# A combined logarithm and exponential table, loaded ahead of the norms and the gate decays of a hybrid decoder step

## The chip, the cores and the metric

The kernel runs on one core of a Trainium2 chip. The metric is the device time in microseconds (us) of one execution; lower is better. The engines of the core are told apart as in the profile: PE is TensorE (PEld its weight loads), DVE is VectorE, ACT is ScalarE, POOL is GpSimd, SP is SyncE, which here only issues transfers.

## The reference, cut to what matters

One decoder layer is computed for a prompt of 256 tokens and for 8 samples of 4 tokens, 288 token columns in all. A state-space branch (four groups) and a gated linear attention branch (GLA, four heads) run in parallel, are merged by sigmoid gates, and are followed by cross-attention and a convolutional feed-forward part. Every matrix product with a weight is float32 in and out. What the change touches are the norms and the logarithm of the GLA gates:

```python
# after the input product, per state-space group of 512 channels
u = u * lax.rsqrt(jnp.mean(u * u, axis=-1, keepdims=True) + EPS)
# per GLA head of 512 channels
o = o * lax.rsqrt(jnp.mean(o * o, axis=-1, keepdims=True) + EPS) * p['gla_norm']
# GLA decays
glog = jax.nn.log_sigmoid((g_lr @ p['w_gla_gate']) + p['b_gla_gate']) / GATE_TAU
# merge, and the norms ahead of cross-attention and of the feed-forward part
merged = jax.nn.sigmoid(gate_a) * branch_a + jax.nn.sigmoid(gate_b) * branch_b
x32 * lax.rsqrt(jnp.mean(x32 * x32, axis=-1, keepdims=True) + EPS)
```

## The kernel before, in words

**The weight products.** All activations are held transposed, channels on the partitions and the 288 tokens along the free axis. `proj_w` takes a weight two row blocks of 128 and 256 columns at a time. Each such piece is one transfer of 256 KB on SP's queue into a ring of six buffers `raw`; `wsplit` rounds it on ACT to `whi` (line 103) and takes the remainder on DVE as `wlo` (line 105), each into a ring of five; then PE runs twelve products of 128x288 on it (lines 148, 149 and 153). This is one step of a main generator. The results lie in two alternating pairs of PSUM tiles, `acc0` and `acc1`; ACT or DVE reads them out when a projection is done.

**The order of the work.** `weave` runs a main generator (projections) and takes, between its steps, steps of a background generator (a scan) in a fixed ratio. Eight units follow each other: four state-space groups, then four GLA heads. During unit `n` the scan of unit `n` is woven into the input projection of unit `n+1` and the output projection of unit `n-1` (`project`). In unit 0 three tile pairs of the half gate `gate_early` stand at the end of the main generator, in unit 2 one more pair; their tangents go to `gq` (line 1275). The program text gives a priority; a scheduler that simulates the engines writes the final order of each engine's queue at build time, apart from instructions that are pinned with `keep_in_program_order`, which puts an instruction behind the one that was traced before it on its engine. In a queue each engine runs in order and waits where an operand is missing.

**The norms.** Each scan ends in `finish`: the sum of squares is split into two parts `sqh` and `sql` (for all but the last unit), PE sums over the partitions with a product with ones (line 989, into a tile of the three-buffer PSUM ring `mm`), and `rstd_from` computes the reciprocal root on ACT as exp(-0.5 ln(x)) in two activations, lines 232 (logarithm) and 233 (exponential). DVE and ACT then make the normed operand `un`, which the output projection uses 16 main steps into the next unit. `rstd_of` does the same for the two full-width norms. The first products of the next scan (lines 761 to 771) take tiles of the same ring `mm`; the third of them takes the one that holds the sum of squares.

**Activation tables.** ACT computes logarithm, exponential, tangent, SiLU and root from a table set that must be loaded; copies, squares, identity and relu need no particular set. The build puts a load ahead of an activation whose function is not in the set that is active, taking a set of its own choice. `S.preload_act_table_set(LNEXP)` is an explicit load of the set named `natural_log_exp_and_others`; the kernel before has one, at its start (line 285). The tangent (lines 650, 658, 1275, 1302 and 1418) serves the SiLU and the sigmoids, and the exponential also the decays of the state-space scan (lines 834, 835) and those of GLA (`decays`, lines 1045 to 1068).

Of the kernel before, what the change touches and what calls it, by code (L numbers as in the profile page):

```python
# [8 lines left out]
F32 = mybir.dt.float32  # L9
# [7 lines left out]
P = 128  # L17
# [6 lines left out]
T = SEQ + NS  # L24
# [12 lines left out]
LNEXP = "natural_log_exp_and_others"  # L37
# [5 lines left out]
def hybrid_step(ctx: ExitStack, tc: tile.TileContext, I: dict, O: list):  # L43
# [3 lines left out]
    V, S, G = nc.vector, nc.scalar, nc.gpsimd  # L47
    MM, TR = nc.tensor.matmul, nc.tensor.transpose

    def pool(name, bufs=1, **kw):  # L50
        return tc.tile_pool(name=name, bufs=bufs, reuse_waits="tile", **kw)

    const = ctx.enter_context(pool("const"))
# [12 lines left out]
    def mm_tile():  # L66
        return ps.tile([P, 512], F32, tag="mm", bufs=3, name="mm")
# [7 lines left out]
    ones = const.tile([P, P], F32, name="ones")  # L75
    V.memset(ones, 1.0)
    epsc = const.tile([P, 3], F32, name="epsc")
    V.memset(epsc[:, 0:1], EPS)
    V.memset(epsc[:, 1:2], 4.0 * EPS)
    fold4 = const.tile([P, NS], F32, name="fold4")  # L80
# [85 lines left out]
    def proj(w, c0, ncol, X, nk, cons, row0=0, alloc=acc_tiles):  # L166
        def load(k0, kn):
            return wload(rows_of(w, row0, k0, kn, c0, ncol))
        return proj_w(load, ncol, X, nk, cons, alloc=alloc)
# [26 lines left out]
    def split_from(hi, lo, src, scale):  # L196
        S.activation(hi, src, ACT.Identity, scale=scale)
        V.scalar_tensor_tensor(lo, src, scale, hi, ALU.mult, ALU.subtract)

    def split(hi, lo, src):  # L200
        S.copy(hi, src)
        V.tensor_tensor(lo, src, hi, ALU.subtract)
# [23 lines left out]

    def two(u, n):
        return lambda k: (u[:, k, :], u[:, n + k, :])

    def rstd_from(pl, ssq, n, four=False):  # L230
        r = pl.tile([P, T], F32, tag="rstd", bufs=1, name="rstd")
        S.activation(r, ssq, ACT.Ln, scale=1.0 / n, bias=epsc[:, 1:2] if four else epsc[:, 0:1])
        S.activation(r, r, ACT.Exp, scale=-0.5)
        return r
# [345 lines left out]
    def a4(name):  # L580
        return pa.tile([P, 4, T], F32, tag="a4", bufs=4, name=name)
# [4 lines left out]
    def b2r(name):  # L586
        return pa.tile([P, 512], F32R, tag="b2", bufs=10, name=name)
# [23 lines left out]
    def e2(name):  # L611
        return pa.tile([P, 2, T], F32, tag="e2", bufs=7, name=name)
# [366 lines left out]
    fin = []  # L979

    def finish(u, sq, gcol, four):

        if len(fin) < 7:
            sp = b2r("sqh")[:, 0:T], b2r("sql")[:, 0:T]
            split(*sp, sq)
            yield
            ssq = mm_tile()
            for w in range(2):
                MM(ssq[:, 0:T], ones.bitcast(F32R), sp[w], start=(w == 0), stop=(w == 1))
        else:  # L990
            ssq = mm_tile()
            MM(ssq[:, 0:T], ones, sq, start=True, stop=True)
        rstd = rstd_from(pa, ssq[:, 0:T], 512, four)
        yield
        un = pa.tile([P, 8, T], F32R, tag="un", bufs=1, name="un")
        for t in range(4):
            V.tensor_tensor(u[:, t, :], u[:, t, :], rstd, ALU.mult)
            split_from(un[:, t, :], un[:, 4 + t, :], u[:, t, :], gcol[:, t:t + 1])
            if t % 2:
                yield  # L1000
        fin.append(un)
# [14 lines left out]
    def gla_proj(h, out):  # L1016
        vT, sr = a4("vT"), a4("sr")
        for j2 in range(2):
            def consv(j, a, j2=j2):
                S.copy(vT[:, 2 * j2 + j, :], a)  # L1020
            yield from proj(I["w_in"], O_V + 512 * h + 256 * j2, 256, X, KT, consv)
        vd = dumped(vT, f"v_d{h}")
        for j2 in range(2):
            def consr(j, a, j2=j2):
                silu2(a, sr[:, j2 * 2 + j, :])
            yield from proj(I["w_in"], O_R + 512 * h + 256 * j2, 256, X, KT, consr)
        eb, qe, ke, kd = e2("eb"), e2("qe"), e2("ke"), e2("kd")
        kde = pa.tile([P, 2, 2, 64], F32, tag="kde", bufs=1, name="kde")
        gw = b2("gw")[:, 0:256]
        for q in (1, 2, 3):  # L1030
            G.dma_start(out=gw[32 * q:32 * q + 16], in_=I["w_gla_gate"][:, 256 * h:256 * h + 256])
        b = kd

        def decays():

            for q in (1, 2, 3):
                S.copy(gw3[32 * q:32 * q + 16], gw[32 * q:32 * q + 16])
            V.tensor_tensor(gw3[96:112], gw[96:112], gw3[96:112], ALU.subtract)
            yield
            for k in range(2):  # L1040
                a = mm_tile()
                MM(a[:, 0:T], gw3[:, k * P:(k + 1) * P], lr3, start=True, stop=True)
                S.activation(qe[:, k, :], a[:, 0:T], ACT.Identity, bias=vec("b_gla_gate")[:, 2 * h + k:2 * h + k + 1])
            yield
            S.activation(ke, qe, ACT.Abs)
            S.activation(ke, ke, ACT.Exp, scale=-1.0)
            S.activation(ke, ke, ACT.Ln, bias=1.0)
            V.scalar_tensor_tensor(qe, qe, 0.0, ke, ALU.min, ALU.subtract)
            yield
            for k in range(2):  # L1050
                V.tensor_tensor_scan(b[:, k, :], rm_g, qe[:, k, :], 0.0, ALU.mult, ALU.add)
            yield
            S.activation(eb, b, ACT.Exp, scale=1.0 / 16.0)
            S.activation(ke, b, ACT.Exp, scale=-1.0 / 16.0)
            for s0, s1, c in ((0, SEQ, 64), (SEQ, T, NL)):
                bv = b[:, :, s0:s1].rearrange("p k (c l) -> p k c l", l=c)
                kv = qe[:, :, s0:s1].rearrange("p k (c l) -> p k c l", l=c)
                for k in range(2):
                    V.tensor_tensor(kv[:, k], bv[:, k, :, c - 1:c].to_broadcast([P, (s1 - s0) // c, c]), bv[:, k],
                                    ALU.subtract)  # L1060
            yield

            for k in range(2):
                bv = b[:, k, 0:SEQ].rearrange("p (i c l) -> p i c l", c=2, l=64)
                V.tensor_tensor(kde[:, k], qe[:, k, 0:SEQ].rearrange("p (i c l) -> p i c l", c=2, l=64)[:, :, 0, :],
                                bv[:, :, 1, 63:64].to_broadcast([P, 2, 64]), ALU.add)
            S.activation(kd, qe, ACT.Exp, scale=1.0 / 16.0)
            S.activation(kde, kde, ACT.Exp, scale=1.0 / 16.0)

        def consq(j, a):  # L1070
            V.scalar_tensor_tensor(qe[:, j, :], a, 1.0 / 16.0, eb[:, j, :], ALU.mult, ALU.mult)

        def consk(j, a):
            V.tensor_tensor(ke[:, j, :], a, ke[:, j, :], ALU.mult)
            V.tensor_tensor(kd[:, j, :], a, kd[:, j, :], ALU.mult)
            V.tensor_tensor(kde[:, j], a[:, 0:SEQ].rearrange("p (i c l) -> p i c l", c=2, l=64)[:, :, 0, :], kde[:, j],
                            ALU.mult)
        dg = decays()
        for _ in proj(I["w_in"], O_K + 256 * h, 256, X, KT, consk):
            next(dg, None)  # L1080
            yield
        yield from proj(I["w_in"], O_Q + 256 * h, 256, X, KT, consq)
        out.append((eb, qe, ke, kd, kde, vT, sr, vd))
# [182 lines left out]
            yield from proj(I["w_in"], o + 256 * j2, 256, X, KT, cons)  # L1266

    gq = []
    GH = KT // 4

    def gate_early(t, a):

        if t % 2 == 0:
            gq.append(e2("gq"))
        S.activation(gq[-1][:, t % 2, :], a, ACT.Tanh, scale=0.5)
        if t % 2:
            G.dma_start(out=ga_d[:, t - 1:t + 1, :], in_=gq[-1])

# [3 lines left out]
    def branch_a(t):  # L1282

        if t < 2 * GH:
            if t % 2 == 0:
# [3 lines left out]
        if t % 4 == 3:  # L1289
            nc.sync.dma_start(out=(mg_d if t < 2 * GH else ma_d)[:, t - 3:t + 1, :], in_=ma[:, t - 3:t + 1, :])  # L1290

# [38 lines left out]
    for n in range(8):  # L1330
        kind, i = units[n]
        scan = (ssd_scan if kind == "s" else gla_scan)(i, *outs[n][0])
        nxt = start(n + 1) if n < 7 else gate(O_GA, gate_a, GH)
        if n == 5:
            mb = bigf("mb")
        parts = [nxt, gate(O_GA, gate_early, 0, GH - 1)] if n == 0 else [steps(nxt, 16), project(n - 1), nxt]
        if n == 2:
            parts.append(gate(O_GA, gate_early, GH - 1, GH))
        weave(chain(*parts), scan, N_MAIN[n], N_BG[n], 20 if n in (2,3) else 0)
# [108 lines left out]

    def rstd_of():
        ssq = mm_tile()  # L1450
        tc.keep_in_program_order(MM(ssq[:, 0:T], ones, rst.pop(), start=True, stop=True))
        return rstd_from(pb, ssq[:, 0:T], D)

    rst = []
# [436 lines left out]
    a = acc_tiles(1)[0]  # L1891
# [64 lines left out]
```

## Time and profile before

| | us |
|---|---|
| three runs: median | 2484.65 |
| three runs: lowest and highest | 2481.55, 2485.2 |
| the profiled execution | 2484.34 |
| its span in the profile | 2482.6 |

The profiled execution lies 0.3 us under the median of the runs. Its time is 1.7 us longer than the span, which goes from the first to the last instruction. The granted TensorE clock was 0.998 over the span. Lines of the profile name the source line, the engine, the operation, the output and input tiles, and then busy time and mean duration; an "idle before" names the engine that ended the wait.

### The profile page before, as it was taken

The numbers are of one execution on the slowest core, as the hardware profiler recorded it, in microseconds if no ns is written. First come the engines' busy times: TensorE is split into PE (matmuls) and PEld (weight loads), VectorE is DVE, ScalarE is ACT, GpSimd is POOL, SyncE is SP. The second block draws the span as 40 slices with busy tenths as digits, with TensorE's granted clock in tenths as the row PEclk, the third lists the DMA queues.
The fourth block names the chain that finished last, engine by engine and source line by source line (L and its number), as shares of the span: only waits on it lengthen the run. The fifth ranks groups of instructions, "written<-read, shape, count | busy, mean of one in ns | idle before, by whom it ended". The sixth has DMA issues, their size and how long they took to land.

```text
span 2482.6 us, 52081 instructions
## 1 busy us (share of the span) xinstructions
PE 2466.9 (99%) x18766; PEld 2387.6 (96%) x18766; DVE 1769.0 (71%) x3794; ACT 1343.4 (54%) x2733; POOL 436.1 (18%) x792
## 2 busy tenths in 40 slices
PE   9999999999999999999999999999999999999998
PEld 8889999999999999999999998999999999999998
DVE  6756778896877666777666577667777676676766
ACT  6656647646464655544555545555555454554545
POOL 3102135143111010110111122402111001020012
PEclk9999999999999999999999999999999999999999
DMA  8877697787769686877777698656555555555555
GB/s 257 250 225 201 167 270 216 205 249 223 230 210 295 200 261 184 249 252 221 234 234 252 204 342 306 195 164 172 170 172 172 172 170 173 170 172 168 170 173 170
DMA packets 457075, 528.66 MB, mean 213 GB/s; under 512 B 40252, under 2 KB 403612, under 8 KB 456784
## 3 DMA queue, kind: packets, MB, share of 16 engines
q1 hardware_dynamic: 420272, 422.39, 56.6%
q0 software_dynamic: 36512, 102.93, 13.0%
q8 instruction: 147, 2.41, 0.4%
q14 instruction: 112, 0.92, 0.1%
q10 hardware_dynamic: 32, 0.01, 0.0%
HBM read 476.41 MB, written 48.76 MB: 212 GB/s over the span
## 4 chain that ended last, share of the span: by engine, by line
PE 95%; DMA 2%; issue 1%; DVE 1%; ACT 0%; POOL 0%; DVEq 0%; POOLq 0%; ACTq 0%
PE acc L149 27%; PE acc L148 27%; PE acc L153 27%; PE acc L328 2%; PE acc L329 2%; PE acc L332 2%; DMA kc<-in_cache_mem_k_dram 1%; PE mm L1239 1%; PE la L1230 1%; PE la L1576 1%; PE mm L1194 0%; DMA raw<-in_w_ssd_out_dram 0%; DMA vc<-in_cache_mem_v_dram 0%; PE la L903 0%; PE mm L924 0%
## 5 line engine op out<-in xcount | busy, mean ns | idle before, releaser
L103 ACT CAST whi<-raw 128x512 fp32r<-128x512 f32 x1464 | 899.7, 618 | 965.2 <-PE acc L149 781.7
L105 DVE TENSOR_TENSOR wlo<-raw,whi 128x512 fp32r<-128x512 f32 x1464 | 996.6, 686 | 549.2 <-ACT whi L103 536.4
L149 PE MATMUL acc<-xn,whi 128*128 128x288 f32 (+1 forms) x1936 | 541.5, 296 | 0.0
L148 PE MATMUL acc<-xn,whi 128*128 128x288 f32 (+1 forms) x1936 | 539.8, 294 | 0.3 <-ACT whi L103 0.3
L153 PE MATMUL acc<-xn,wlo 128*128 128x288 f32 (+1 forms) x1936 | 408.2, 292 | 0.0
L149 PE MATMUL acc<-hf,whi 128*128 128x288 f32 x1408 | 393.1, 296 | 0.0
L148 PE MATMUL acc<-hf,whi 128*128 128x288 f32 x1408 | 388.7, 292 | 0.0
L148 PEld LDWEIGHTS acc<-xn,whi 128*128 128x128 f32 (+1 forms) x1936 | 363.3, 188 | 5.1 <-issue 2.3
L149 PEld LDWEIGHTS acc<-xn,whi 128*128 128x128 f32 (+1 forms) x1936 | 363.7, 188 | 3.6 <-issue 0.4
L153 PEld LDWEIGHTS acc<-xn,wlo 128*128 128x128 f32 (+1 forms) x1936 | 310.4, 188 | 0.9 <-issue 0.4
L153 PE MATMUL acc<-hf,wlo 128*128 128x288 f32 x1408 | 294.5, 290 | 0.0
L149 PEld LDWEIGHTS acc<-hf,whi 128*128 128x128 f32 x1408 | 264.5, 188 | 0.0
L148 PEld LDWEIGHTS acc<-hf,whi 128*128 128x128 f32 x1408 | 264.0, 188 | 0.0
L153 PEld LDWEIGHTS acc<-hf,wlo 128*128 128x128 f32 x1408 | 226.3, 188 | 0.1
L149 PE MATMUL acc<-pr,whi 128*128 128x288 f32 x704 | 196.6, 295 | 0.0
L148 PE MATMUL acc<-pr,whi 128*128 128x288 f32 x704 | 194.8, 293 | 0.0
L1749 POOL COPY fsp<-fst 128x16 f32<-128x16 f32 x88 | 37.3, 427 | 650.7 <-DVE av L1761 431.4
L153 PE MATMUL acc<-pr,wlo 128*128 128x288 f32 x704 | 147.3, 290 | 0.0
L148 PE MATMUL acc<-un,whi 128*128 128x288 f32 x512 | 143.0, 295 | 2.5 <-ACT vT L1020 1.5
L149 PE MATMUL acc<-un,whi 128*128 128x288 f32 x512 | 142.9, 295 | 0.0
L149 PEld LDWEIGHTS acc<-pr,whi 128*128 128x128 f32 x704 | 132.3, 188 | 0.0
L148 PEld LDWEIGHTS acc<-pr,whi 128*128 128x128 f32 x704 | 132.0, 188 | 0.0
(551 smaller groups left out, 4301.9 us busy)
## 6 DMA issues: line engine op xcount, KB each, us to landing
raw<-in_w_in_dram SPq DMA_DIRECT2D x480, 256.0 KB
raw<-in_w_up_dram SPq DMA_DIRECT2D x352, 256.0 KB
raw<-in_w_down_dram SPq DMA_DIRECT2D x176, 256.0 KB
raw<-in_w_ck_dram SPq DMA_DIRECT2D x64, 256.0 KB
raw<-in_w_cv_dram SPq DMA_DIRECT2D x64, 256.0 KB
raw<-in_w_ssd_out_dram SPq DMA_DIRECT2D x64, 256.0 KB
sin<-in_state_gla_dram POOLq DMA_DIRECT2D x32, 512.0 KB, 6.2
out_dram<-sin SPq DMA_DIRECT2D x32, 512.0 KB
```

Source lines behind the costliest of these rows:

```text
L103: S.copy(hi, raw)
L105: V.tensor_tensor(lo, raw, hi, ALU.subtract)
L148: MM(a, hi[:, k, cs], xh, start=(k0 + s0 + k == 0), stop=False)
L149: MM(a, hi[:, k, cs], xl, start=False, stop=False)
L153: MM(a, lo[:, k, cs], xh, start=False, stop=(k0 + s0 + k == nk - 1))
L328: MM(accs[m], mn_hi[:, kk, ms_], hi[:, 0, :], start=(kk == 0), stop=False)
L329: MM(accs[m], mn_lo[:, kk, ms_], hi[:, 0, :], start=False, stop=False)
L332: MM(accs[m], mn_hi[:, kk, ms_], lo[:, 0, :], start=False, stop=(kk == KT - 1))
L1230: MM(osa[NS * j:NS * j + NS, :], qdm[:, k, b, :], sins[b][:, k, :], start=False, stop=(q == 1 and k == 0))
L1239: MM(a, kb[:, k * P:(k + 1) * P], vst, start=True, stop=True)
L1576: MM(ssc[NS * c:NS * c + NS, 0:P], xq[:, j, u, :], kt[:, j], start=(j == 0), stop=(j == 15))
L1749: G.tensor_copy(sp[:, :, 0:2], st.rearrange("p (b k) -> p b k", k=2))
```

## The change

A new helper `lnexp` loads the combined set explicitly. With an operand it first copies one column of it to a new scratch tile `junk1`, so that the load stands behind whatever wrote that operand. It is called in three places: in `finish` for the first seven units, behind the product with ones; in `decays`, between the absolute value and the first exponential; and in `rstd_of`, ahead of the product with ones. In `finish` of units 0 and 2 a loop is added that gives way to the main generator until the next pair of half-gate tangents has been traced, and the copy reads the last of them; in the other units it reads `sql`.

```diff
+    junk1 = const.tile([P, 1], F32, name="junk1")
...
+    def lnexp(after=None):
+
+        if after is not None:
+            S.copy(junk1, after)
+        tc.keep_in_program_order(S.preload_act_table_set(LNEXP))
...
     # finish
             for w in range(2):
                 MM(ssq[:, 0:T], ones.bitcast(F32R), sp[w], start=(w == 0), stop=(w == 1))
+            if len(fin) in (0, 2):
+                after = len(gq)
+                while len(gq) == after or len(tanhs) % 2:
+                    yield
+                lnexp(gq[-1][:, 1, 0:1])
+            else:
+                lnexp(sp[1][:, 0:1])
...
     # decays
             S.activation(ke, qe, ACT.Abs)
+            lnexp()
             S.activation(ke, ke, ACT.Exp, scale=-1.0)
             S.activation(ke, ke, ACT.Ln, bias=1.0)
...
     gq = []
+    tanhs = []
...
     # gate_early
         S.activation(gq[-1][:, t % 2, :], a, ACT.Tanh, scale=0.5)
+        tanhs.append(t)
...
     def rstd_of():
         ssq = mm_tile()
-        tc.keep_in_program_order(MM(ssq[:, 0:T], ones, rst.pop(), start=True, stop=True))
+        a = rst.pop()
+        lnexp(a[:, 0:1])
+        tc.keep_in_program_order(MM(ssq[:, 0:T], ones, a, start=True, stop=True))
```

## The prediction

> **What bounds the kernel now.** I read the head of the page first, then the waits of PE, then PE's idle time in windows, and only then the table loads on ACT, which are what the change is about.
>
> ```profile
> span 2482.6 us, 52081 instructions
> PE 2466.9 (99%) x18766; PEld 2387.6 (96%) x18766; DVE 1769.0 (71%) x3794; ACT 1343.4 (54%) x2733; POOL 436.1 (18%) x792
> ...
> PE 95%; DMA 2%; issue 1%; DVE 1%; ACT 0%; POOL 0%; DVEq 0%; POOLq 0%; ACTq 0%
> ```
>
> PE is busy for 2466.9 of 2482.6 us and carries 95% of the chain that ended last. The change takes no work from PE, so all that it can win is inside the 15.7 us in which PE is idle. ACT is idle for nearly half the span: a shorter ACT is worth nothing unless PE stood waiting for it. So the next view is what PE waited for, over the whole span (engine, line, releaser: us, times, longest).
>
> ```profile
> PE acc L148 <- ACT vT L1020: 1.5, 2, 1.1
> ...
> PE acc L148 <- DVE ma L1010: 1.0, 1, 1.0
> PE mm L771 <- ACT rstd L232: 0.8, 1, 0.8
> PE acc L148 <- ACT whi L103: 0.3, 1, 0.3
> ```
>
> Only one of these waits names a norm: line 771 waited once, 0.8 us, for the logarithm of line 232. The windows say where the idle time lies (stretch, its length, PE busy, PEld, DVE, ACT, POOL, clock, DMA share).
>
> ```profile
> 0.00:40.00 40.00, 38.87 (x191) 32.64 (x192) 27.38 (x67) 27.89 (x63) 18.61 (x50) 1.00 0.80 245
> ...
> 2440.00:2482.00 42.00, 33.21 (x261) 32.97 (x259) 25.51 (x49) 20.97 (x41) 9.63 (x15) 0.91 0.56 157
> ```
>
> ```profile
> 480.00:500.00 20.00, 19.17 (x149) 18.88 (x148) 18.86 (x41) 15.87 (x32) 0.61 (x1) 1.00 0.45 136
> ...
> 585.00:605.00 20.00, 19.69 (x154) 19.41 (x153) 14.30 (x31) 18.83 (x44) 8.75 (x13) 1.00 0.61 176
> 605.00:625.00 20.00, 18.52 (x145) 17.91 (x145) 11.73 (x23) 9.32 (x20) 13.59 (x21) 1.00 1.02 279
> 625.00:645.00 20.00, 19.02 (x165) 18.04 (x160) 19.63 (x44) 6.13 (x11) 5.19 (x9) 1.00 0.64 190
> 660.00:680.00 20.00, 20.00 (x156) 19.16 (x158) 12.03 (x23) 10.09 (x19) 0.00 (x0) 1.00 0.80 233
> 680.00:700.00 20.00, 20.00 (x158) 18.99 (x148) 16.66 (x41) 15.58 (x26) 5.18 (x8) 1.00 0.59 155
> 775.00:800.00 25.00, 25.00 (x188) 23.11 (x187) 16.18 (x28) 11.26 (x22) 3.86 (x7) 1.00 0.99 297
> ```
>
> Start (1.13 us) and tail (8.79 us) hold 9.9 of the 15.7 us, and nothing of the change is there. Of the other 5.8 us, 0.83 lie in the stretch of norm 1 (480 to 500), 0.31 + 1.48 + 0.98 = 2.77 behind norm 2 (585 to 645). Around the first GLA decays and norm 3 (680 to 700) PE has no idle time at all. The most that the whole change can win is therefore about 5.8 us, 0.23%.
>
> **The change part by part.** First the loads themselves (line, count, busy us, mean ns).
>
> ```profile
> L232 ACT ACT_TABLE_LOAD x10 | 12.8, 1283 | 0.2
> L233 ACT ACT_TABLE_LOAD x10 | 12.8, 1283 | 0.2
> ...
> L1047 ACT ACT_TABLE_LOAD x4 | 5.1, 1283 | 0.1
> L1053 ACT ACT_TABLE_LOAD x4 | 5.1, 1283 | 0.1
> ...
> L650 ACT ACT_TABLE_LOAD x1 | 1.3, 1283 | 0.0
> ...
> L286 ACT COPY epsc<-epsc 128x1 f32<-128x1 f32 x1 | 0.2, 191 | 0.0
> ```
>
> Each of ten norms loads for the logarithm and again for the exponential, each of four decays likewise: 28 loads, and four others (lines 285, 650, 1799, 1824) make 32. The set that the exponential brings holds the tangent too: no tangent loads, but the first one at line 650, which stands behind the combined set loaded at the start. So the combined set lacks the tangent, and after the change the first tangent behind a norm must load again. Counting the program: start 1, first tangent 1, decays 4, norms 0 to 6 seven, the two norms of `rstd_of` 2, norm 7 (whose branch has no `lnexp`) 2, tangents behind norms 0 to 6 seven, SiLU and root 2: 26 loads. If a preload of the set already active is dropped, norms 3 to 6 and the second `rstd_of` save five: 21. ACT thus saves 6 to 11 loads of 1.283 us and gets nine copies of about 0.19 us (price from line 286): 6 to 12 us net of 1343 us. That total is hidden; what counts is where the load sits.
>
> Norm 1, on DVE, PE and ACT (start, us, instruction, wait before it):
>
> ```profile
> 485.42 0.45 DVE L202 TENSOR_TENSOR sql<-sqa,sqh 128x288 fp32r<-128x288 f32 x1
> ...
> 488.22 1.28 ACT L232 ACT_TABLE_LOAD   x1
> ...
> 488.36 0.38 PE L989 MATMUL mm<-sql,ones 128*128 128x288 f32 x1
> ...
> 489.51 0.50 ACT L232 ACTIVATE rstd<-mm,epsc 128x288 f32<-128x288 f32 x1
> ...
> 490.07 0.33 PE L771 MATMUL mm<-ident,xsT 128*128 128x128 f32 x1 [0.83 <-ACT rstd L232]
> ```
>
> The sum of squares is complete at 488.74, the logarithm starts at 489.51, because the load runs until 489.50. The new copy needs `sql`, there at 485.87, so copy and load (1.47 us) can be through by 488; the logarithm then starts 0.77 us earlier and PE's wait shrinks by that. Queued behind copy and load are the weight casts of line 103, which PE needs several pieces later; I cost that at nothing. Term A: -0.8 us (bounds: 0 if the load stays behind the product, -0.83 at most).
>
> Norm 2, on ACT, with the last half-gate tangent and the stalls behind:
>
> ```profile
> 586.87 0.40 ACT L1275 ACTIVATE gq<-acc 128x288 f32<-128x288 f32 x1
> ...
> 588.56 1.28 ACT L232 ACT_TABLE_LOAD   x1
> 589.85 0.50 ACT L232 ACTIVATE rstd<-mm,epsc 128x288 f32<-128x288 f32 x1
> ...
> 591.54 1.28 ACT L233 ACT_TABLE_LOAD   x1
> 592.84 0.44 ACT L233 ACTIVATE rstd<-rstd 128x288 f32<-128x288 f32 x1
> ...
> 601.08 0.60 ACT L103 CAST whi<-raw 128x512 fp32r<-128x512 f32 x1
> ...
> 618.77 0.62 ACT L103 CAST whi<-raw 128x512 fp32r<-128x512 f32 x1 [3.43 <-DMA raw<-in_w_ssd_out_dram]
> 619.30 0.39 ACT L1020 COPY vT<-acc 128x288 f32<-128x288 f32 x1
> 620.95 0.62 ACT L103 CAST whi<-raw 128x512 fp32r<-128x512 f32 x1 [1.27 <-DMA raw<-in_w_ssd_out_dram]
> 621.48 0.39 ACT L1020 COPY vT<-acc 128x288 f32<-128x288 f32 x1
> ```
>
> From 588.56 to 608 ACT has not one gap: here it is the bound. The cast at 601.08 comes too late (PE's 0.3 us wait for `whi`), and because casts free the `raw` ring late, the transfers of the next projection are issued late and bunch up in a stretch whose DMA share is 1.02; two casts wait for them, and the `vT` copies queued behind these casts keep PE waiting 1.5 us for its accumulators. The norm already stands behind the tangent (586.87), so the new loop moves nothing; the first load stays where it is, and the second (591.54) goes. Everything behind it moves 1.28 us ahead, less one copy (0.19): 1.1. PE can follow by no more than that: 0.3 at the cast and the rest, 0.8 of 1.5, at the copies. The next wait, 1.0 us on `ma`, ends with a chain of transfers that moves with the rest. Term B: -1.1 us (bounds: 0 if the transfers come no earlier, -1.8 if both stalls vanish).
>
> Norm 0:
>
> ```profile
> 371.91 0.40 ACT L1275 ACTIVATE gq<-acc 128x288 f32<-128x288 f32 x1
> 372.33 1.28 ACT L232 ACT_TABLE_LOAD   x1
> 373.63 0.50 ACT L232 ACTIVATE rstd<-mm,epsc 128x288 f32<-128x288 f32 x1
> ```
>
> It too follows the last tangent at once, so the wait added there costs the copy alone, and PE shows no wait for this logarithm. The transfers of the gate pair are issued ahead of the loop as before; SP's and POOL's queues get nothing new. Norms 3 to 6, the decays and both `rstd_of`: PE idles at none of them, a shorter ACT is worth 0.
>
> The seven tangents that now reload are all behind `acc` or `cva`; the GLA ones stand in stretches like 660 to 680 and 775 to 800, where PE is never idle and ACT is busy 10.09 of 20 and 11.26 of 25 us. What each holds up is the release of one accumulator pair, wanted again one whole projection later. I take 0, with 1.3 us each as the upper bound.
>
> The sum: A -0.8, B -1.1, others 0: -1.9 us against the profiled 2484.34, which makes 2482.4; against the median of the runs, 0.3 higher, 2482.75. I say 2482.6.
>
> [...]
>
> **The rivals.** *Nothing moves.* The scheduler leaves the load of norm 1 behind the product, or the transfers at 605 to 625 are set by the DMA share of 1.02 and not by their issue. For it: that share, and that the three waits in question hold 2.6 us in all (0.8, 1.5, 0.3). Against it: the casts there did free `raw` late. Time 2484.5.
>
> *The freed ACT time unblocks more.* All of the 0.83 us and of the 2.77 us behind norm 2 go, the 0.98 us of 625 to 645 too: -3.6, 2481.0. That is what a switch worth more than its 1.28 us would do. Against it: 1.30 us from load to activation. [...] A gain over 5 us would need nearly all 5.8 us and is left almost no chance.
>
> *Reloads exposed: slower.* The tangent of each unit now waits for a load that was not there. [...] If PE waits for each of the seven, that is 7 x 1.30 = 9.1 us less 1.9: 2491.8. It decides from two exposed reloads on (2.6 against 1.9), and is over 0.2% from six on. For it: ACT runs in order, so the casts behind the tangent wait as well, and the DMA share is 0.99 in 775 to 800. Against it: idle ACT time and whole projections of slack. A rewritten queue order, which the trace of before cannot show, has the same sign and size.
>
> **How the numbers follow.** Forecast (-0.8 to -3): 0.55. Nothing moves: 0.24. More freed: 0.08. Exposed reloads or a worse order: 0.13, about half of it over 5 us. 0.2% is 5 us, about what a measurement of this kernel can tell from no change; the three runs already differ by 3.7. Faster by more than that 0.05 (an upper end of "more freed"), slower by more 0.08, within it 0.87. The range: the forecast and "more freed" with the runs' scatter give the low end, 2479.5; a few exposed reloads the high end, 2487.5.
>
> **What would show it.** Loads: 21 to 26 instead of 32, none left at line 1047, 1053 or, in norms 0 to 6, 233. Term A: PE's wait at line 771 for the logarithm falls under 0.2 us, with the load over before the product with ones ends. Term B: ACT from the norm 2 load to its first gap 1 us shorter, PE's wait for `vT` under 0.8 and for `whi` gone. Reloads: ACT loads at the first tangents near 396, 509, 663, 779, 898, 1016 and 1076, with PE full around them. I am wrong if PE's idle time outside start and tail is not about 3.9 us, or if a tangent slips between a preload and its logarithm, which would show as three loads in one norm.

## The result, and the profile after

The changed kernel takes 2500.86 us (median of 6 runs, 2497.86 to 2509.82) against 2483.78 us for the kernel before (6 runs, 2481.55 to 2485.8): a ratio of 1.0074, with a 95% interval of 1.006 to 1.0087. It is 17 us slower. The forecast was 2482.6 us, and its range ended at 2487.5.

The profiled execution of the changed kernel took 2506.51 us, 5.6 us more than its median, so its rows show somewhat more loss than a typical run has. The head of its page, its largest DMA queue (packets, MB, share of 16 engines) and its chain:

```profile
span 2504.6 us, 52086 instructions
...
PE 2476.7 (99%) x18766; PEld 2394.7 (96%) x18766; DVE 1769.6 (71%) x3794; ACT 1335.3 (53%) x2736; POOL 437.8 (17%) x792
...
q1 hardware_dynamic: 420272, 422.39, 57.7%
...
PE 92%; DMA 5%; DVE 1%; issue 1%; ACT 0%; POOL 0%; DVEq 0%; ACTq 0%; POOLq 0%; SPq 0%
```

The same queue in the kernel before:

```profile
q1 hardware_dynamic: 420272, 422.39, 56.6%
```

ACT does what the change says: it is 8.1 us less busy (1343.4 before). The engines' own instructions aren't slower: DVE is busy for 1769.6 us (1769.0 before), and a weight cast on ACT takes 620 ns (619 before). What is new is the DMA side. Packets and megabytes are the same to the last digit, and yet they occupy a larger share of a span that is itself longer. DMA has risen from 2% to 5% of the chain that ended last. PE is idle for 27.9 us instead of 15.7. Its waits after the change (engine, line, releaser: us, times, longest):

```profile
PE acc L149 <- ACT whi L104: 4.1, 2, 3.2
PE la L1652 <- DVE pms L1639: 3.5, 2, 2.4
PE acc L149 <- DVE ma L1024: 3.4, 2, 2.6
PE mm L931 <- ACT cst L632: 3.1, 1, 3.1
PE acc L149 <- ACT vT L1034: 1.2, 1, 1.2
...
PE mm L778 <- ACT rstd L239: 1.0, 1, 1.0
```

The first five have nothing to do with a norm. The last is the wait at the third tile of norm 1 (line 771 before): it was to go, and it has become 0.14 us longer (0.97 instead of 0.83). Where the time goes is in the windows (stretch, length, PE, PEld, DVE, ACT, POOL, clock, DMA share, GB/s). First the kernel before:

```profile
200.00:372.00 172.00, 172.00 (x1343) 169.17 (x1342) 126.31 (x257) 97.38 (x208) 47.65 (x96) 1.00 0.76 214
372.00:600.00 228.00, 227.17 (x1784) 220.95 (x1783) 188.13 (x407) 144.16 (x317) 81.95 (x144) 1.00 0.77 220
...
560.00:600.00 40.00, 40.00 (x311) 38.15 (x310) 25.72 (x51) 25.37 (x56) 11.33 (x18) 1.00 0.71 201
...
680.00:1150.00 470.00, 470.00 (x3541) 450.26 (x3531) 333.23 (x686) 255.99 (x471) 54.92 (x84) 1.00 0.76 235
...
1400.00:1560.00 160.00, 158.43 (x1631) 144.13 (x1630) 114.20 (x284) 77.52 (x185) 37.38 (x55) 1.00 0.85 300
```

and the changed kernel:

```profile
200.00:372.00 172.00, 171.08 (x1323) 167.32 (x1323) 124.66 (x255) 95.34 (x204) 47.60 (x96) 1.00 0.79 208
372.00:600.00 228.00, 220.57 (x1682) 212.18 (x1681) 179.38 (x388) 131.12 (x288) 76.69 (x132) 0.99 0.82 211
...
560.00:600.00 40.00, 36.80 (x261) 34.68 (x260) 26.51 (x56) 17.77 (x34) 4.72 (x7) 0.91 0.83 234
...
680.00:1150.00 470.00, 470.00 (x3542) 449.74 (x3541) 333.87 (x681) 251.12 (x468) 54.38 (x83) 1.00 0.78 236
...
1400.00:1560.00 160.00, 155.86 (x1607) 144.96 (x1605) 112.69 (x274) 77.26 (x179) 30.70 (x44) 1.00 0.86 290
```

Read the counts of PE in brackets. From 372 to 600 us PE gets through 1682 matmuls instead of 1784; at the pace of before (228 / 1784 = 0.128 us each), that is 13 us lost in one stretch. 6.6 us of it are idle time that was not there (7.4 against 0.8); the rest is spent in slower products, some 3.6 us of it between 560 and 600, where the granted clock is 0.91 (0.09 x 40 us) and was 1.00. From 680 to 1150 us the counts are equal: no time is lost at the GLA norms and decays. Product against product (each matmul against the one with the same number in the kernel before), the changed kernel is 17.9 us behind at 680 us of the kernel before, 17.8 at 1150 and 22.1 from 1560 on. So most of the loss lies in the state-space stretch, and some 4 us more in cross-attention between 1150 and 1560, where PE waits 3.5 us for `pms`. DMA carries fewer GB/s at a higher share (211 at 0.82 against 220 at 0.77).

The first row matters most. From 200 to 372 us, ahead of the first instruction that the change adds, PE is already 20 matmuls short. On every engine the order of instructions up to there is the same in the two traces. What ACT waited for there and behind (200 to 680 us; before, then after):

```profile
ACT whi L103 <- DMA raw<-in_w_in_dram: 19.6, 17, 2.5
```

```profile
ACT whi L104 <- DMA raw<-in_w_in_dram: 55.3, 35, 5.6
```

The casts of these weight pieces wait 55.3 us for their transfers instead of 19.6, and up to 5.6 us at a time. Norm 0, where the new code runs first (start, us, instruction):

```profile
374.38 0.40 ACT L1291 ACTIVATE gq<-acc 128x288 f32<-128x288 f32 x1
374.82 0.19 ACT L234 COPY junk<-gq 128x1 f32<-128x1 f32 x1
375.03 1.28 ACT L235 ACT_TABLE_LOAD   x1
376.32 0.50 ACT L239 ACTIVATE rstd<-mm,epsc 128x288 f32<-128x288 f32 x1
```

The tangent ahead of the copy starts at 374.38; before, it was at 371.91. So the kernel is 2.5 us late *before* it has done anything new. Neither a table load nor a queue can be the reason for that. One thing of the change acts from the first transfer on: the line that allocates `junk1`.

### The profile page after: what moved, and what is told of

The parts are those of the page before. It is cut to its first block, busy times and chain, and to the rows that moved or that the text cites. A ratio compares the mean times of both kernels' runs of the same rounds, so it can differ in the third digit from the quotient of the medians.

```text
span 2504.6 us, 52086 instructions
## 1 busy us (share of the span) xinstructions
PE 2476.7 (99%) x18766; PEld 2394.7 (96%) x18766; DVE 1769.6 (71%) x3794; ACT 1335.3 (53%) x2736; POOL 437.8 (17%) x792
## 4 chain that ended last, share of the span: by engine, by line
PE 92%; DMA 5%; DVE 1%; issue 1%; ACT 0%; POOL 0%; DVEq 0%; ACTq 0%; POOLq 0%; SPq 0%
PE acc L150 26%; PE acc L149 26%; PE acc L154 26%; PE acc L335 2%; PE acc L339 2%; PE acc L336 2%; DMA raw<-in_w_in_dram 2%; DMA raw<-in_w_ssd_out_dram 1%; DMA kc<-in_cache_mem_k_dram 1%; PE mm L1254 1%; PE la L1245 1%; PE la L1595 1%; DMA sqr<-in_state_ssd_dram 0%; PE mm L1209 0%; PE la L1652 0%
```

## The experiments

The theory: `junk1` costs the time, not the loads. It stands in the first pool, so the program's address list has 187 of its 195 SBUF names 32 bytes higher (4 bytes per partition, allocated as 32): the weight pieces `raw` go from byte 18688 (73 x 256) to 18720. The rivals: the loads cost it (or the order they bring), or both do. All ratios below are against the kernel before on the same chip, with 95% intervals; the kernel before had medians of 2485.16 (15 runs), 2483.24 (11) and 2483.61 us (26) in the three sets.

**The tile alone.** The kernel before, plus the tile and nothing else:

```
+    junk1 = const.tile([P, 1], F32, name="junk1")
+    V.memset(junk1, 0.0)
```

> The kernel before plus the scratch tile junk1 alone (128x1 float32, filled once by DVE); no table load, no loop, no copy is added. Nearly every SBUF tile lies 32 bytes higher by it, raw at 18720 instead of 18688. Theory ADDRESS (the loss is made by that shift, in transfers that start 32 bytes off a 64-byte boundary): about 2500 us, 1.005 to 1.009 of before, transfers of 4096 bytes on POOL's queue with a median over 200 ns between 200 and 600 us as in the changed kernel (174 ns before). Theory ORDER (the loss is made by the new order on ACT and DVE or by the table loads): 2484 us, 0.999 to 1.001.

2506.56 us, 1.0086 [1.0071, 1.0101]. The orders on PE, ACT and SP are those of the kernel before, no load has moved, and the whole loss is there: 21.4 us. The 4096-byte packets of POOL's queue have a median of 226 ns between 200 and 600 us (174 before, 226 after the change), as the theory had it.

**The change without the tile.** The changed kernel, with the scratch in a spare column:

```
-    epsc = const.tile([P, 3], F32, name="epsc")
-    junk1 = const.tile([P, 1], F32, name="junk1")
+    epsc = const.tile([P, 4], F32, name="epsc")
+    junk1 = epsc[:, 3:4]
```

> The whole change, but its scratch column is an unused column of the tile epsc, so no tile is added and no address of a ring moves (raw at 18688). Theory ADDRESS: the loss is gone and the forecast of the prediction holds, 2480 to 2484 us, about 1.9 us under before (0.9985 to 1.0003). Theory ORDER: as slow as the changed kernel, 2497 to 2505 us (1.005 to 1.009).

2482.9 us (11 runs, 2480.54 to 2485.57), 0.9992 [0.9983, 1.0001]. The loss is gone. ACT's wait for the same weights is back near that of before (20.5 us there over the whole span), against 64.2 us in the changed kernel. First this kernel, then the changed one:

```profile
ACT whi L104 <- DMA raw<-in_w_in_dram: 27.4, 25, 3.2
```

```profile
ACT whi L104 <- DMA raw<-in_w_in_dram: 64.2, 42, 5.6
```

So 1.0074 / 0.9992 = 1.0082, 20 us, is the price of 32 bytes in the changed kernel, and 21.4 us in the kernel before. What the change does with the tables is worth -2.3 us by the medians, and its interval includes no change.

**Which tiles?** Two kernels divide the 187 names. One takes 32 bytes out ahead of the weight ring and puts them behind it, so that only `raw`, `whi` and `wlo` move (by -32). The other puts the 32 bytes between that ring and the rest, so that the ring stays and 178 names move.

```
+    pad = ctx.enter_context(pool("pad"))        # behind the pool of the ring
-    alog = const.tile([32, 1], F32, name="alog")
+    alog = pad.tile([32, 1], F32, name="alog")
```

> The kernel before with one constant tile (32 bytes) moved from ahead of the weight rings to behind them: raw, whi and wlo lie 32 bytes lower (raw at 18656), all later tiles where they were. If under theory ADDRESS the weight transfers into raw make the loss, all or most of the 17 us are here (2495 to 2501 us); if the other destinations (states, squares, keys, values) make it, 2484 to 2487 us. Theory ORDER: 2484 us.

```
+    pad = ctx.enter_context(pool("pad"))        # behind the pool of the ring
+    junk1 = pad.tile([P, 1], F32, name="junk1")
+    V.memset(junk1, 0.0)
```

> The kernel before with a 32-byte tile put between the weight rings and everything behind them: raw, whi and wlo stay, the other 178 names lie 32 bytes higher. Theory ADDRESS: the rest of the 17 us that the run with the rings alone does not show; if the weight transfers make it all, 2484 us; if the states, squares, keys and values make it, 2495 to 2501 us. Theory ORDER: 2484 us.

The ring alone: 2528.73 us, 1.0177 [1.0163, 1.0191]. The rest alone: 2539.46, 1.0223 [1.0209, 1.0237]. Both lose more than the shift of everything, which neither theory had foreseen. What explains it are the windows of the feed-forward stretch, where PE is never idle. The kernel before, the ring alone and the rest alone, in this order:

```profile
1700.00:2400.00 700.00, 700.00 (x5387) 700.00 (x5386) 502.48 (x1179) 360.08 (x772) 78.95 (x162) 1.00 0.57 171
```

```profile
1700.00:2400.00 700.00, 700.00 (x5252) 700.00 (x5251) 493.15 (x1168) 352.39 (x765) 79.70 (x166) 1.00 0.57 167
```

```profile
1700.00:2400.00 700.00, 700.00 (x5253) 700.00 (x5252) 493.31 (x1168) 353.70 (x766) 82.28 (x170) 1.00 0.58 167
```

5387 matmuls in 700 us are 129.9 ns each, 5252 are 133.3. PE waits for nothing and its clock is 1.00; each product itself is slower. It is the `wlo` products above all. In the page's groups (busy, mean ns), before and then with the ring moved:

```profile
L153 PE MATMUL acc<-hf,wlo 128*128 128x288 f32 x1408 | 294.5, 290 | 0.0
```

```profile
L154 PE MATMUL acc<-hf,wlo 128*128 128x288 f32 x1408 | 302.9, 298 | 0.0
```

The kernel before and the changed one both have 5387 there: the effect appears when weights and activations are moved *against each other*, and not when they move together. It costs 43.6 us alone (the ring alone: 2528.73 - 2485.16), and there is next to no transfer loss in that kernel: ACT's wait for the same weights is 26.6 us (20.5 before), and PE's waits are close to those of before.

```profile
PE acc L149 <- ACT vT L1021: 1.0, 1, 1.0
PE mm L772 <- ACT rstd L233: 0.8, 1, 0.8
```

With the rest moved, by contrast, both effects are there: the same 5253 products, and 48.1 us of ACT's waits for `raw`, although `raw` lies where it lay before.

```profile
ACT whi L106 <- DMA raw<-in_w_in_dram: 48.1, 30, 5.6
```

So `raw` is the victim: moved alone it comes hardly later, and left in place it comes late, because *other* transfers, in the tiles behind the ring, have moved.

**How far may a tile be moved?** The tile alone, of 64 and of 128 bytes:

```
+    junk1 = const.tile([P, 16], F32, name="junk1")   # 64 bytes; [P, 32] for 128
+    V.memset(junk1, 0.0)
```

> The kernel before plus a scratch tile of 64 bytes instead of 32 (128x16 float32, filled once): nearly every tile lies 64 bytes higher, raw at 18752, which is a multiple of 64 but not of 256. If a transfer loses by straddling 64-byte lines, the loss of the 32-byte tile (21 us) is gone: 2484 to 2487 us. [...]

> The kernel before plus a scratch tile of 128 bytes: nearly every tile lies 128 bytes higher, a multiple of 128 but, for raw and the state tiles, not of 256. If transfers lose by crossing 128-byte lines: 2484 to 2487 us, as before. If by not starting at a multiple of 256 bytes: 2499 to 2507 us, as with 32 and 64.

64 bytes: 2503.6 us, 1.008 [1.0065, 1.0095], as bad as 32. 128 bytes: 2490.3 us (9 runs), 1.0025 [1.0014, 1.0036], 6.7 us, a third of the loss: neither forecast's number. The rest alone moved by 64 and by 128 bytes, the tile standing in `pad`:

```
+    junk1 = pad.tile([P, 16], F32, name="junk1")     # 64 bytes; [P, 32] for 128
+    V.memset(junk1, 0.0)
```

> The kernel before with a 64-byte tile between the weight rings and the rest: weights stay, activations lie 64 bytes higher. With 32 bytes there each product of 128x288 took 133.3 ns instead of 129.9. If what counts is whether weights and activations agree modulo 64 bytes: 129.9 ns again and 2484 to 2487 us. If it is a larger modulus: 133 ns or another value, 2520 us or more; a value under 129.9 ns would make the kernel faster than before.

> The kernel before with a 128-byte tile between the weight rings and the rest: weights stay, activations lie 128 bytes higher. One look, for the spacing of the products. If weights and activations must agree modulo 128 bytes: 129.9 ns, about 2485 to 2500 us. If modulo 256: 133 ns as with 32 and 64 bytes, about 2530 us.

2537.34 us, 1.0215 [1.02, 1.0231] for 64; a single run of 2524.68 us for 128, and its products are slow too (here the latter):

```profile
1700.00:2400.00 700.00, 700.00 (x5252) 700.00 (x5252) 493.99 (x1169) 352.53 (x764) 79.97 (x166) 1.00 0.57 166
```

That suggested a period of 256 bytes for the products. Four constants of 256 bytes together moved from ahead of the ring to behind it, so that the ring moves by -256 and nearly all else stays (two other constants, `vcol` and `scw`, move by 128):

```
-    fold4 = const.tile([P, NS], F32, name="fold4")
+    fold4 = pad.tile([P, NS], F32, name="fold4")
...
-    dcol, dtb, alog = const.tile(...), const.tile(...), const.tile(...)
+    dcol, dtb, alog = pad.tile(...), pad.tile(...), pad.tile(...)
```

> The kernel before with four constant tiles (256 bytes) moved from ahead of the weight rings to behind them: raw, whi and wlo lie 256 bytes lower, nearly everything else stays. If 256 bytes is the period of both effects: 129.9 ns a product and 2482 to 2487 us, as before. If the period is longer: 133 ns and over 2520 us, as with the ring 32 bytes lower.

2483.68 us (10 runs), 1.0003 [0.9993, 1.0012], and products as fast as before:

```profile
1700.00:2400.00 700.00, 700.00 (x5387) 700.00 (x5386) 502.58 (x1179) 360.02 (x771) 78.71 (x162) 1.00 0.58 171
```

**Which transfers?** The squares of the state, `sqr`, are loaded in pieces that fill part of a tile. The kernel before with these loads 32 bytes further into their tile, where they are then read as well, everything else in place; and the 32-byte tile with the same edit, which brings `sqr` back to a multiple of 64 bytes (from byte 144000 before to 144064):

```
-            sq_ = e2("sqr").rearrange("p a t -> p (a t)")[:, 0:512]
+            sq_ = e2("sqr").rearrange("p a t -> p (a t)")[:, 8:520]
```

> The kernel before with the 128 square loads of the state (sqr, pieces of 128 bytes) written and read 8 columns (32 bytes) into their tile; no address of a tile moves. If these loads make the transfer loss of the 32-byte tile: 2498 to 2506 us, with PE waiting for vT, cst and whi between 540 and 660 us. If the large state loads and stores (sin) or the rest make it: 2484 to 2488 us.

> The kernel before plus the 32-byte tile (2506.6 us), with the square loads alone put back on a multiple of 64 bytes (8 columns into their tile). If these loads make the loss: back to 2484 to 2490 us. If not: 2500 to 2507 us. Between the two, the part that is theirs.

The squares alone cost 7.5 us: 2490.73 us (8 runs), 1.0031 [1.0021, 1.0042], between its two forecasts. ACT's wait for the same weights over the whole span is 41.4 us here (20.5 before, 64.2 after the change), and PE waits for `whi` and `vT`:

```profile
ACT whi L103 <- DMA raw<-in_w_in_dram: 41.4, 28, 3.7
```

```profile
PE acc L148 <- ACT whi L103: 3.6, 3, 2.9
PE acc L148 <- ACT vT L1020: 3.0, 2, 2.2
```

So a destination that is 32 bytes off is enough, without any other tile moved. Brought back, the squares win nothing: 2504.04 us, 1.0081 [1.0064, 1.0099] instead of 1.0086. They are then on a multiple of 64, but not where they were modulo 128 or 256, so this run can't tell "other transfers carry the loss" from "64 isn't enough". The 64-byte shift, in which every tile keeps its place modulo 64 and the loss is whole, speaks for the second.

**Term A on its own.** In the kernel without the shift, norm 1 still loads late, because the copy waits for `sql`. Here norms 1 and 3 to 6 load without the copy, as soon as their square is split:

```
+            if len(fin) not in (0, 2):
+                lnexp()
...
-            else:
-                lnexp(sp[1][:, 0:1])
```

> The change without a shift, and in the norms other than 0 and 2 the load is pinned right behind the cast to sqh, without the copy: two weight casts earlier, and with no wait for sql. The copy put the load behind sql, and so behind the product, which is why PE still waited 1.0 us at the third tile of norm 1. Theory: that wait goes, about 0.9 us less than the change without a shift, 2480 to 2483.5 us, 0.9980 to 0.9995 of before, and PE's wait for the logarithm under 0.2 us. Rival: the casts that now stand behind the load come later and PE waits for whi instead: no difference to the change without a shift.

2483.46 us (11 runs), 1.0 [0.9991, 1.0008]. What it shows of term A stands in the next section.

## Why the prediction was wrong

**The step that failed** is the list of the change's parts. It went through loads, copies, queues, the loop and the tangents, and left out the line `junk1 = const.tile(...)`. A tile of 4 bytes was costed at nothing, without saying so and without asking what it moves. The runs put 21.4 us on that line alone (1.0086), and without it the change stands at 0.9992. The rival that ended on the other side had the right sign and the wrong cause: neither the reloads nor the order of the queues costs the time, and even its price, 2491.8 us, ends 9 us short. In its first 372 us the changed kernel has the order of the kernel before. The forecast's 2482.6 us is nearly what the kernel without the shift takes (2482.9), but that is the time of another kernel, and luck in part: of the two terms behind it, A did not come and B isn't shown.

**The loads** came out as counted. After the change (line, count, busy us, mean ns):

```profile
L235 ACT ACT_TABLE_LOAD x13 | 16.7, 1283 | 0.2
L665 ACT ACT_TABLE_LOAD x4 | 5.1, 1283 | 0.1
L657 ACT ACT_TABLE_LOAD x3 | 3.8, 1283 | 0.1
...
L1319 ACT ACT_TABLE_LOAD x1 | 1.3, 1283 | 0.0
```

With norm 7's two and three single ones there are 26, the upper end of 21 to 26: thirteen preloads, none dropped, and eight ahead of tangents (lines 657, 665 and 1319: the first one, which was there before, and seven reloads). **The reloads** stay hidden: no wait of PE, in the changed kernel or without the shift, names a tangent's accumulator. Only PE's weight loads wait for one, without the shift three times and 2.5 us in all (once and 0.8 us before), while products run. And a switch costs its load alone here: from the load's start at 375.03 to the logarithm at 376.32 us in norm 0 is 1.29 us, and the load takes 1.28.

**Term A (-0.8 us)** put the load ahead of the product. In the kernel without the shift it isn't there (start, us, instruction, wait):

```profile
488.72 0.45 DVE L203 TENSOR_TENSOR sql<-sqa,sqh 128x288 fp32r<-128x288 f32 x1
...
489.38 0.19 ACT L234 COPY epsc<-sql 128x1 f32<-128x1 f32 x1
...
489.58 1.28 ACT L235 ACT_TABLE_LOAD   x1
...
489.57 0.38 PE L996 MATMUL mm<-sql,ones 128*128 128x288 f32 x1
...
491.43 0.66 PE L778 MATMUL mm<-ident,xsT 128*128 128x128 f32 x4 [0.98 <-ACT rstd L239]
```

The prediction took `sql` to be there 2.5 us before the product, as in the old trace. In the new schedule DVE is done with the last sum of squares at 486.07 (483.13 before), and one more gate product (`sz`) stands ahead of `sql`; `sql` is there at 489.17 (485.87 before), and copy and load run beside the product instead of ahead of it. PE's wait is 0.98 us (0.83 before): the term is 0 or slightly worse. This was the lower bound that the prediction gave, but its value was the other end. The kernel with the early load shows that the mechanism itself is sound. Its ACT in norm 1:

```profile
487.14 0.44 ACT L202 CAST sqh<-sqa 128x288 fp32r<-128x288 f32 x1
487.59 1.28 ACT L235 ACT_TABLE_LOAD   x1
...
490.14 0.50 ACT L239 ACTIVATE rstd<-mm,epsc 128x288 f32<-128x288 f32 x1
```

The load is over at 488.87 and PE no longer waits for a logarithm in its table of waits. But nothing of it reaches the time (1.0 [0.9991, 1.0008]): in the profiled execution, the slowest of the 11, PE waits 2.8 us for `vT` instead.

**Term B (-1.1 us)** is not shown. The second load of norm 2 is gone, and without the shift PE waits 0.2 us for `vT` and not for `whi` (1.5 and 0.3 before):

```profile
PE acc L149 <- ACT vT L1034: 0.2, 1, 0.2
```

That is as forecast. But the kernel with the ring at -256, whose tables are those of before, has the same 0.2 us at `vT`, and 1.1 and 1.9 us at `whi` and `ma`:

```profile
PE acc L149 <- DVE ma L1011: 1.9, 1, 1.9
PE acc L149 <- ACT whi L104: 1.1, 2, 0.8
...
PE acc L149 <- ACT vT L1021: 0.2, 1, 0.2
```

These waits vary by some 2 us from kernel to kernel whatever the tables do, so a single profile can't carry a term of 1 us there. Product against product, the profile without the shift wins 2.1 us on the kernel before between 600 and 680 us, and the one with the early load, whose norm 2 is the same, loses 2.0 there. The median difference of -2.3 us is compatible with the sum of -1.9 us and with nothing.

**What stays open**: which transfers besides the squares carry the other 14 us, if the losses add (the state's loads and stores or the keys and values; each alone wasn't tried), and why 128 bytes cost a third.

## What to carry to other kernels

A new tile is an edit to every address behind it: when a diff allocates, look up what moves, and put scratch into a spare column or behind everything else. Keep weights and activations relative to each other where a tuned kernel has them (here 32, 64 or 128 bytes between them made the feed-forward products 133.3 ns instead of 129.9, and 256 left them at 129.9), and what DMA writes where it is: for the transfers, a common shift by 32, 64 and 128 bytes cost 21.4, 20.4 and 6.7 us here, and a shift of the tiles behind the ring by 256 wasn't tried. A shift of 32 bytes cost this kernel between 0.3% and 2.2%. When a trace is late before the first changed instruction, stop reading instructions and compare addresses.

## What the runs showed of the hardware

*Transfers and addresses.* A common shift of nearly all tiles costs 21.4 us at 32 bytes, 20.4 at 64 and 6.7 at 128. The weight ring alone loses next to no transfer time, at -256 as at -32 (ACT waits 23.2 and 26.6 us for it, 20.5 before). The fastest packet isn't slower: of the 4096-byte packets of queue q0 (POOL's), the fastest take some 159 ns in every kernel. But between 372 and 680 us their mean, over the trace's packet records, is 225 ns before, 225 with the ring alone, 262 with the tile alone and 268 after the change, and the packets at 159 ns fall from 1300 of 3712 to 365 of 3744. From 1400 to 1700 us, with 7424 such packets in each kernel, the median is 159 ns before and with the ring alone, 171 with the tile alone and after the change, 168 with 64 bytes and 167 with 128. So most of them take some 8 to 12 ns longer there; whether that, or transfers that disturb one another, makes the weights late is not shown. The 1024-byte packets of queue q1, most of them weight pieces, have a median of 46 ns in every kernel, wherever `raw` lies. How an address makes a packet longer, no run shows.

*Products and addresses.* When weights and activations are moved against each other by 32, 64 or 128 bytes, the feed-forward products take 133.3 ns instead of 129.9 (5252 or 5253 in 700 us instead of 5387); moved together by 32, 64 or 128, or the ring alone by 256, they take 129.9 as before. The longer products are 43.6 us of this kernel with the ring alone at -32, twice the loss under study, from 32 bytes.
